# Seven block products in all four feed-forwards of a YOCO decoder step; state updates and gate sums at other places

## The chip, the cores and the metric

One core of a Trainium2 chip runs the whole program in one launch. The metric is the device time of one execution in microseconds (us), lower is better. Of each kernel there are several timed executions, and one profiled execution with a trace of every instruction on the five engines: PE (TensorE), DVE (VectorE), ACT (ScalarE), POOL (GpSimd), SP (SyncE, which here only issues DMAs).

## The reference

One inference step of a two-layer decoder, for 512 prompt tokens and 8 sequences of 4 new tokens. Layer 0 mixes by gated linear attention (GLA), layer 1 by forgetting attention (FoX) on keys and values that are projected once, after layer 0. Cut to what matters:

```python
D_MODEL, D_FF = 1024, 2816
def swiglu(u, w_up, w_down):
    a, b = jnp.split(u @ w_up, 2, axis=-1)
    return (jax.nn.silu(a) * b) @ w_down
for layer in range(2):
    mod = (silu(c) @ w_ada[layer] + b_ada[layer]).reshape(Bn, 3, 3, 1024)
    u = modulate(h, g[layer, 0], mod[:, 0, 0], mod[:, 0, 1])        # rmsnorm, scale, shift
    h = h + 0.5 * mod[:, 0, 2] * swiglu(u, w_ffn_up[layer, 0], w_ffn_down[layer, 0])
    u = modulate(h, g[layer, 1], mod[:, 1, 0], mod[:, 1, 1])
    h = h + mod[:, 1, 2] * (gla_mixer(u) if layer == 0 else fox_mixer(u, kv))
    u = modulate(h, g[layer, 2], mod[:, 2, 0], mod[:, 2, 1])
    h = h + 0.5 * mod[:, 2, 2] * swiglu(u, w_ffn_up[layer, 1], w_ffn_down[layer, 1])
    if layer == 0:
        kv = shared_kv(h, ...)              # K (normed), V and log forget values of all tokens
# GLA state of each sequence and head after its 4 tokens, 128 x 256:
#   S = exp(b_last) * S + k_decayed^T v
# FoX scores get cumulative sums of the log forget values
```

All is float32.

## The kernel before

The residual stream `h` stays in SBUF, features on partitions: `[128, 8, 544]`, 544 tokens = 512 + 32, worked on in two halves of 272. A float32 product is made of three matmuls on the high and low parts of both sides (`acc3`, L176 high x high, L177 low of the first x high, L178 high x low of the second); ACT makes the high parts by a cast (`halves`, L157), DVE the low parts by a subtraction (L158). So `u` lives as `uh` and `ul`, a weight as `hua` and `lua` and the like.

The program is one chain of stages. Times are from the trace, from the span's start: FFN "00" 31.4 to 475.8 us, GLA to 767, FFN "02" 768.2 to 1216.1, keys and values ("kv") 1217.9 to 1329.6, FFN "10" 1329.7 to 1733.3, FoX 1734.8 to 2036, FFN "12" 2037.4 to 2420.4, then the output.

An FFN has 22 pairs of 128 columns (`a` and `b` of SwiGLU). "00", "02" and "10" use `ffn`: for each pair and half, `pa` and `pb` (8 x 3 matmuls of 128x128 by 272 each), the gate, and the down products of groups of pairs (2, then 4 each), whose result `pd` is added into `h` with its gate (L393; the last 32 tokens by L396 and, on POOL, L398). "12" uses `ffn_seven`: the first 3 pairs as before, the other 19 by seven block products in place of eight. The operand of a pair is seen as a 2 x 2 block matrix (two halves of the features by two halves of the tokens) and the weights as 2 x 2 (features by `a` and `b`). Sums of blocks of `u` are made once, ahead of pair 3 (L534, L527; their high and low parts `th`, `tl`; the last of them is written over a quarter of `uh`, `ul` by `last_input`); sums of weights for each pair (`s`, L611, L612, L617, L618 on POOL); the seven products are combined on DVE and ACT (L643 to L680: `u`, `a`, `c`), and the gated result's low part `gl` is made on POOL (L649). Pairs go in rounds of 3, 3, 3, 3, 3, 3, 2, 2. While a round's products run, the down blocks of the round before are put between them (`between`); 16 blocks a round.

What else rides on the FFNs: "00" and "02" have the conditioning vectors (`ada_seq`, nine vectors each, matmuls `ada` in runs of 32 with their weight loads `adaw` of 512 KB on SP); "02" has also 16 `state_step`, which update the sample sequences' GLA states: two matmuls `pus` and two DVE updates `s` in each, with a masked key tile `km` (POOL) for every head, the state read by SP, and the result written by a DMA that POOL issues. "10" has four steps of gate work: logarithms of the forget gates (`gate_logs`, ACT), a transpose and running sum (`gate_turn`), sums at block borders (`gate_tiles`) and those of the cached pages (`gate_pages`). After the last block of a half, `after_half` makes the norm and the `u` of that half for the next stage (`nv`, `uh`, `ul`; L367, L386, L387).

In "kv", `proj_tokens` walks five chunks of columns by five token tiles (four of 128, one of the 32 samples), with the evacuation of a unit (norm of the keys, `hxk`, scaled on POOL, transposed on PE, split) one unit behind it.

The Tile framework's scheduler sets the order on each engine from the order of the code and of the dependences; tile pools with a count of buffers set how far ahead a load can run.

Of the kernel before, what the change touches and what calls it, by code (L numbers as in the profile page):

```python
# [99 lines left out]
def trunk_kernel(ctx: ExitStack, tc: tile.TileContext, a, out, dbg=None, stop=None):  # L100
# [19 lines left out]
    def raw_tile(name, dt=F32):  # L120
        return wp.tile([P, 1056], dt, tag="raw", name=name, bufs=4)

    def hi_tile(name, dt=F32R):
        return wp.tile([P, 1056], dt, tag="hi", name=name, bufs=6)

    def lo_tile(name, dt=F32R):
        return wp.tile([P, 1056], dt, tag="lo", name=name, bufs=6)
# [52 lines left out]
    def apply_u(ps, w, half, k0=0, k1=NB):  # L180
        t0, t1 = HALF[half]
        acc3(ps[:, 0:HA], [(w[0][:, k], w[1][:, k], uh[:, k, t0:t1], ul[:, k, t0:t1]) for k in range(k0, k1)], k0 == 0, k1 == NB)

# [147 lines left out]
    def spread(name, y, pieces):  # L331
        diag = tmp.tile([P, 3, P], F32, tag="diag", name=f"diag{name}", bufs=1)
# [175 lines left out]
    def ffn_seven(name, l, s, gate, after_half, steps=(), final=False, plain=3):  # L508
        wu = a["w_ffn_up"][l, s]
        wd = a["w_ffn_down"][l, s]  # L510
        steps = list(steps)
# [6 lines left out]
        with tc.tile_pool(name="ffn" + name, bufs=1) as fp:  # L518
            th, tl = ({i: fp.tile([P, H2, HA], F32R, name=f"t{x}{i}{name}") for i in (1, 2, 4)} for x in "hl")
            t3 = fp.tile([P, H2, HA], F32, name=f"t3{name}")  # L520
# [14 lines left out]

            def inputs():
                for k in range(H2):
                    x1, x2 = (tmp.tile([P, HA], F32, tag="nv", name=f"x{i}{name}_{k}", bufs=3)[:] for i in (1, 2))
                    x3 = t3[:, k]
# [6 lines left out]
                    minus(x3, x2, x3)  # L546
                    minus(x2, x2, x1)
                    halves(th[2][:, k], tl[2][:, k], x2)
                    x4 = tmp.tile([P, HA], F32, tag="nv", name=f"x4{name}_{k}", bufs=3)[:]
# [16 lines left out]
            def g_tiles(q):  # L566
                gt[q] = (fp.tile([P, T], F32R, tag="gh", name=f"gh{name}_{q}", bufs=6),
                         fp.tile([P, T], F32R, tag="gl", name=f"gl{name}_{q}", bufs=6))
# [8 lines left out]
            def plain_up(q, half):  # L577
                t0, t1 = HALF[half]
# [3 lines left out]
                apply_u(pb, wt[q][1], half)  # L582
                g = tmp.tile([P, HA], F32, tag="sq", name=f"g{name}_{q}_{half}", bufs=3)
                S.activation(g[:], pa[:, 0:HA], AF.Silu)
                V.tensor_tensor(out=g[:], in0=g[:], in1=pb[:, 0:HA], op=ALU.mult)
                halves(gt[q][0][:, t0:t1], gt[q][1][:, t0:t1], g[:])

# [63 lines left out]
            def seven(q, between):  # L651
# [32 lines left out]
                if steps:  # L684
                    steps.pop(0)()
# [34 lines left out]
            for q in range(2):  # L720
                plain_weights(q)
            plain_up(0, 0)
            plain_up(1, 0)
            plain_up(0, 1)
# [21 lines left out]
            for r in range(1, len(rounds)):  # L746
                todo = blocks(r - 1)
                n, done = 7 * len(rounds[r]), [0]

                def between():  # L750
                    done[0] += 1
                    while len_out[0] < 2 * NB * done[0] // n:
                        next(todo)
                        len_out[0] += 1
                len_out = [0]
# [4 lines left out]
            r = len(rounds) - 1  # L760
            for half in range(2):
                for m in range(NB):
                    down_block(r, m, half, True)
                    if half == 0 and m % 2 == 0:
                        down_weights(r, m // 2 + 1) if m < NB - 2 else None
                after_half(half)
# [92 lines left out]
    def proj_tokens(name, w2d, chunks, evac, evac_s, last=(0, 1, 4, 2, 3)):  # L859
# [28 lines left out]
        for ci, pieces in enumerate(chunks):  # L888
# [7 lines left out]
            for i, t in enumerate(order):  # L896
                if ci < len(chunks) - 1 and i == 3:
# [95 lines left out]
    def late_masks():  # L993
# [4 lines left out]
    ffn("00", 0, 0, mod(0, 0, 2), after("01", mod(0, 1, 0), mod(0, 1, 1)),  # L998
        seq0[:-2] + [late_consts, late_masks], first=(w00, feed), held=seq0[-2:])
# [5 lines left out]
    gsv = ExitStack()  # L1005
    gs_pool = gsv.enter_context(tc.tile_pool(name="gsv", bufs=1))
    vs = gs_pool.tile([P, 256], F32, name="vs")
    kts = gs_pool.tile([P, P], F32, name="kts")
    ebl = gs_pool.tile([P, 4, 12], F32, name="ebl")
# [315 lines left out]
    def state_stacks():  # L1325
# [13 lines left out]
    def state_step(hd, bh, pr):  # L1339
        if bh == 0 and pr == 0:  # L1340
            if hd == 0:
                state_stacks()
# [4 lines left out]
        if pr == 0:  # L1347
            t = gs_pool2.tile([P, 1024], F32, tag="s1", name=f"s1_{hd}_{bh}", bufs=1)
            stk["s"] = t[:].rearrange("p (b e) -> p b e", b=4)
            SP.dma_start(out=stk["s"], in_=a["state_gla"][0, 4 * bh:4 * bh + 4, hd].rearrange("b d e -> d b e"))  # L1350
        st = stk["s"]
# [6 lines left out]
        if pr:  # L1358
            G.dma_start(out=out[6][0, 4 * bh:4 * bh + 4, hd].rearrange("b d e -> d b e"), in_=st)

    with tc.tile_pool(name="gsv2", bufs=1) as gs_pool2:
        st_steps = [lambda hd=hd, bh=bh, pr=pr: state_step(hd, bh, pr) for hd in range(4) for bh in range(2) for pr in range(2)]
        seq = []
        seq1 = ada_seq(range(11, 20))
        for i, s in enumerate(seq1[:-2]):
            seq.append(s)
            if i >= 2 and st_steps:
                seq.append(st_steps.pop(0))
        ffn("02", 0, 1, mod(0, 2, 2), after("kv", 72, 80), seq + st_steps, held=seq1[-2:])
    gsv.close()  # L1370
# [43 lines left out]
    gates = ExitStack()  # L1414
    gt_pool = gates.enter_context(tc.tile_pool(name="gate", bufs=1))
    lf = gt_pool.tile([P, 5, 16], F32, name="lf")
    with tc.tile_pool(name="kvt", bufs=1) as kp:
# [39 lines left out]

        nv = {(hf, k): kp.tile([P, HA], F32, name=f"nv10_{hf}_{k}") for hf in range(1) for k in range(NB)}
        left = proj_tokens("kv", a["w_kvf"], [[(0, 512)], [(512, 512)], [(1024, 352)], [(1376, 352)], [(1728, 320), (2048, 16)]], evac_kv, evac_kvs, (4, 0, 1, 2, 3))
# [7 lines left out]
    le = gt_pool.tile([P, 5, 16], F32, name="le")  # L1467
    lt = gt_pool.tile([16, TP], F32, name="lt")
    rs = gt_pool.tile([16, TP], F32, name="rs")
    loc = gt_pool.tile([16, TP], F32, name="loc")  # L1470
    loc2 = gt_pool.tile([16, 2, TP], F32R, name="loc2")
    off = gt_pool.tile([16, 4, 4, 1], F32, name="off")
    off2 = gt_pool.tile([16, 2, 16], F32R, name="off2")
    gsm = gt_pool.tile([16, 16, P], F32, name="gsm")
    lp = gt_pool.tile([P, 2, 8, 16], F32, name="lp")
    lne = gt_pool.tile([32, 8, 16], F32, name="lne")

    def gate_logs():
        S.activation(le[:], lf[:], AF.Abs)
        S.activation(le[:], le[:], AF.Exp, scale=-1.0)  # L1480
        S.activation(le[:], le[:], AF.Ln, bias=1.0)
        V.tensor_scalar(out=lf[:], in0=lf[:], scalar1=0.0, scalar2=None, op0=ALU.min)
        V.tensor_tensor(out=lf[:], in0=lf[:], in1=le[:], op=ALU.subtract)
# [359 lines left out]
```

## Time and profile before

| | us |
|---|---|
| runs | 2422.88, 2429.81, 2434.22 (median 2429.81) |
| profiled execution | 2429.69, of it the span 2427.9; TensorE clock 0.989 of full |
| FFN "00", "02", "10" (plain) | 444.4, 447.9, 403.6 |
| FFN "12" (seven products) | 383.0 |
| GLA; FoX | 289; 301 |
| keys and values | 112 |

Rows in the profile read: line, engine, operation, tiles out<-in, shape, count | busy us, mean ns of one | idle time before them and what ended it. Rows of stretches give for each engine its busy us and instructions, the granted TensorE clock, the share of time in which the DMA engines were busy, and GB/s.

### The profile page before, as it was taken

The page shows a single profiled execution, that of the slowest core. Times are in us where ns is not written, and L with a number is a line of the kernel's source. Part 1 is how long each engine was busy: PE and PEld are TensorE (multiplying, and loading weights), DVE is VectorE, ACT ScalarE, POOL GpSimd, SP SyncE. Part 2 cuts the span into 40 slices and gives each one's busy share as a digit, 9 for nine tenths or more (in the row PEclk, how much of TensorE's full clock was granted, in tenths as well). Part 3 has the DMA queues.
Part 4 walks back from the last instruction along what each step waited for, and adds up shares of the span by engine and source line. Part 5 has one row for each costly group of instructions (what it writes and reads, how often), then busy time and mean ns, then how long its engine had stood idle before and what let it go on. Part 6 is the DMA issues. An engine that isn't in the chain of part 4 may idle for free.

```text
span 2427.9 us, 48518 instructions
## 1 busy us (share of the span) xinstructions
PE 2362.8 (97%) x19976; PEld 2215.4 (91%) x19976; DVE 1381.7 (57%) x3082; ACT 832.4 (34%) x1529; POOL 443.5 (18%) x574
## 2 busy tenths in 40 slices
PE   7999999998999999999999999999998899999999
PEld 6999999997979999999979999999896569999999
DVE  6343343548556453443585345344766666888887
ACT  3212222334534222221334323222435544444432
POOL 0000000206202010100120000000224212355442
PEclk8999999998999999999999999999999999999999
DMA  9636444322262645446337423222136751233322
GB/s 304 213 124 220 163 159 155 111 60 63 60 191 88 216 158 187 167 152 207 131 116 226 120 70 110 88 87 88 44 88 160 189 166 53 77 94 96 98 86 77
DMA packets 334131, 319.40 MB, mean 132 GB/s; under 512 B 24767, under 2 KB 287773, under 8 KB 333862
## 3 DMA queue, kind: packets, MB, share of 16 engines
q1 hardware_dynamic: 320134, 304.44, 39.5%
q0 software_dynamic: 13776, 11.87, 2.3%
q8 instruction: 157, 2.57, 0.4%
q14 instruction: 64, 0.52, 0.1%
HBM read 298.17 MB, written 18.38 MB: 130 GB/s over the span
## 4 chain that ended last, share of the span: by engine, by line
PE 82%; DVE 9%; DMA 4%; ACT 2%; POOL 2%; issue 1%; SPq 0%; ACTq 0%; DVEq 0%; POOLq 0%
PE pd L178 7%; PE pd L176 7%; PE pd L177 7%; PE pa L176 6%; PE pb L178 5%; PE pb L177 5%; PE pa L177 5%; PE pa L178 5%; PE pb L176 5%; PE p L177 3%; PE p L178 3%; PE p L176 3%; PE ada L231 3%; DMA kd<-khscr 2%; DVE nv L367 1%
## 5 line engine op out<-in xcount | busy, mean ns | idle before, releaser
L176 PE MATMUL pa<-uh,hua 128*128 128x272 f32 x1104 | 323.0, 293 | 1.8 <-ACT uh L386 1.7
L177 PE MATMUL pa<-ul,hua 128*128 128x272 f32 x1104 | 321.3, 291 | 0.4 <-DVE ul L387 0.2
L178 PE MATMUL pa<-uh,lua 128*128 128x272 f32 x1104 | 320.0, 290 | 0.0
L178 PE MATMUL pb<-uh,lub 128*128 128x272 f32 x1104 | 319.3, 289 | 0.0
L177 PE MATMUL pb<-ul,hub 128*128 128x272 f32 x1104 | 318.8, 289 | 0.0
L176 PE MATMUL pb<-uh,hub 128*128 128x272 f32 x1104 | 318.3, 288 | 0.0
L393 DVE SCALAR_TENSOR_TENSOR h<-pd,mods,h 128x272 f32<-128x272 f32 (+1 forms) x416 | 199.7, 481 | 194.8 <-PE pd L178 193.9
L178 PE MATMUL pd<-gh,lwd 128*128 128x272 f32 x1056 | 305.1, 289 | 0.0
L176 PE MATMUL pd<-gh,hwd 128*128 128x272 f32 x1056 | 305.0, 289 | 0.0
L177 PE MATMUL pd<-gl,hwd 128*128 128x272 f32 x1056 | 304.8, 289 | 0.0
L398 POOL TENSOR_TENSOR h<-h,gs 128x32 f32<-128x32 f32 x208 | 81.3, 391 | 941.4 <-DVE gs L396 936.0
L176 PEld LDWEIGHTS pa<-uh,hua 128*128 128x128 f32 x1104 | 208.9, 189 | 14.6 <-issue 6.0
L177 PEld LDWEIGHTS pa<-ul,hua 128*128 128x128 f32 x1104 | 209.3, 190 | 1.7 <-DVE ul L387 1.4
L178 PEld LDWEIGHTS pa<-uh,lua 128*128 128x128 f32 x1104 | 209.0, 189 | 0.0
L177 PEld LDWEIGHTS pb<-ul,hub 128*128 128x128 f32 x1104 | 209.0, 189 | 0.0
L176 PEld LDWEIGHTS pb<-uh,hub 128*128 128x128 f32 x1104 | 208.9, 189 | 0.0
L178 PEld LDWEIGHTS pb<-uh,lub 128*128 128x128 f32 x1104 | 208.7, 189 | 0.0
L446 DVE TENSOR_TENSOR g<-g,pb 128x272 f32<-128x272 f32 x132 | 57.7, 437 | 262.8 <-PE pb L178 261.4
L176 PEld LDWEIGHTS pd<-gh,hwd 128*128 128x128 f32 x1056 | 199.4, 189 | 1.7 <-issue 1.6
L177 PEld LDWEIGHTS pd<-gl,hwd 128*128 128x128 f32 x1056 | 199.3, 189 | 0.0
L178 PEld LDWEIGHTS pd<-gh,lwd 128*128 128x128 f32 x1056 | 199.1, 189 | 0.0
L157 ACT CAST hua<-rua 128x1024 fp32r<-128x1024 f32 x69 | 72.3, 1048 | 355.7 <-PE pd L177 264.2
(551 smaller groups left out, 5822.5 us busy)
## 6 DMA issues: line engine op xcount, KB each, us to landing
adaw<-in_w_ada_dram SPq DMA_DIRECT2D x128, 512.0 KB, 5.9
rua<-in_w_ffn_up_dram SPq DMA_DIRECT2D x88, 512.0 KB, 3.9
rub<-in_w_ffn_up_dram SPq DMA_DIRECT2D x88, 512.0 KB, 4.3
rwd<-in_w_ffn_down_dram SPq DMA_DIRECT2D x66, 512.0 KB, 5.0
rd<-in_w_ffn_down_dram SPq DMA_DIRECT2D x24, 384.0 KB, 3.3
adah<-in_w_ada_dram SPq DMA_DIRECT2D x16, 512.0 KB, 7.7
adaw<-in_w_ada_kv_dram SPq DMA_DIRECT2D x16, 512.0 KB, 6.4
s<-in_state_gla_dram SPq DMA_DIRECT2D x16, 512.0 KB, 4.4
```

Source lines behind the costliest of these rows:

```text
L157: S.copy(hi, src)
L176: PE.matmul(ps, lhsT=wh, rhs=xh, start=first and i == 0, stop=False)
L177: PE.matmul(ps, lhsT=wh, rhs=xl, start=False, stop=False)
L178: PE.matmul(ps, lhsT=wl, rhs=xh, start=False, stop=last and i == n - 1)
L231: PE.matmul(ps[32 * j:32 * j + 32, 0:256], lhsT=sc[:, k, :], rhs=t[:, j * 256:(j + 1) * 256], start=k == 0, stop=k == NB - 1)
L367: V.scalar_tensor_tensor(out=v[:, 0:p1 - t0], in0=h[:, k, t0:p1], scalar=mods[:, scale + k, 0:1], in1=rb[:, t0:p1], op0=ALU.mult, op1=ALU. ...
L393: V.scalar_tensor_tensor(out=h[:, m, t0:p1], in0=ps[:, 0:n], scalar=mods[:, gate + m, 0:1], in1=h[:, m, t0:p1], op0=ALU.mult, op1=ALU.add)
L398: G.tensor_tensor(out=h[:, m, TP:T], in0=h[:, m, TP:T], in1=st[:], op=ALU.add)
L446: V.tensor_tensor(out=g[:], in0=g[:], in1=pb[:, 0:HA], op=ALU.mult)
```

## The change

All four FFNs call `ffn_seven`. "00" and "02" call it with `slots=5` (tiles of gated results for five pairs, not six) and `late=True`: the fourth sum of blocks isn't kept from `inputs()` but made again in `last_input`, block by block. With `slots=5` the 16 down blocks of the last round are spread over the first 14 products of a round, so the first comes behind the first product, also in rounds with 21; with six, over all of a round's products. The conditioning steps are handed out by `tick()` after each product. The state updates go to "kv", one `state_step` a unit from the second on; the states are read through POOL's queue, two buffers ahead (`state_load`), the first two ahead of the stage. The gate work goes to FoX, to the units of its output gate. Smaller: raw, high and low weight tiles 1056 to 1040 wide, and the diagonal tile of `spread` shares a buffer.

Core of the diff:

```diff
-    def ffn_seven(name, l, s, gate, after_half, steps=(), final=False, plain=3):
+    def ffn_seven(name, l, s, gate, after_half, steps=(), final=False, first=None, held=(), slots=6, late=False):
...
+        total, ticks, n_ticks = len(steps), [0], 2 * plain + 7 * (NQ - plain)
+        def tick():
+            ticks[0] += 1
+            for _ in range(max(total * ticks[0] // n_ticks, min(total, ticks[0], 4)) - (total - len(steps))):
+                steps.pop(0)()
...
-            t3 = fp.tile([P, H2, HA], F32, name=f"t3{name}")
+            t3 = None if late else fp.tile([P, H2, HA], F32, name=f"t3{name}")
...
             def last_input():
-                S.copy(quarter(uh, 0, 1), t3[:])
-                minus(quarter(ul, 0, 1), t3[:], quarter(uh, 0, 1).bitcast(F32))
+                if not late:
+                    S.copy(quarter(uh, 0, 1), t3[:])
+                    minus(quarter(ul, 0, 1), t3[:], quarter(uh, 0, 1).bitcast(F32))
+                    return
+                for k in range(H2):
+                    x2, x3 = short(5, k), short(6, k)
+                    plus(x2, 1, 1, k)
+                    plus(x3, 0, 1, k)
+                    minus(x2, x2, x3)
+                    t0, t1 = HALF[1]
+                    halves(uh[:, k, t0:t1], ul[:, k, t0:t1], x2)
...
-                n, done = 7 * len(rounds[r]), [0]
+                n, done, gone = min(7 * len(rounds[r]), 7 * (slots - 3)), [0], [0]
...
-    def proj_tokens(name, w2d, chunks, evac, evac_s, last=(0, 1, 4, 2, 3)):
+    def proj_tokens(name, w2d, chunks, evac, evac_s, last=(0, 1, 4, 2, 3), extra=()):
...
             for i, t in enumerate(order):
+                if extra and ci + i:
+                    extra.pop(0)()
...
-    ffn("00", 0, 0, mod(0, 0, 2), after("01", mod(0, 1, 0), mod(0, 1, 1)),
-        seq0[:-2] + [late_consts, late_masks], first=(w00, feed), held=seq0[-2:])
+    ffn_seven("00", 0, 0, mod(0, 0, 2), after("01", mod(0, 1, 0), mod(0, 1, 1)),
+              seq0[:-2] + [late_consts, late_masks], first=(w00, feed), held=seq0[-2:], slots=5, late=True)
...
+    def state_load(gs_pool2, i):
+        if i < 8:
+            hd, bh = divmod(i, 2)
+            t = gs_pool2.tile([P, 1024], F32, tag="s1", name=f"s1_{hd}_{bh}", bufs=2)
+            stk["s", i] = t[:].rearrange("p (b e) -> p b e", b=4)
+            G.dma_start(out=stk["s", i], in_=a["state_gla"][0, 4 * bh:4 * bh + 4, hd].rearrange("b d e -> d b e"))
...
         if pr:
             G.dma_start(out=out[6][0, 4 * bh:4 * bh + 4, hd].rearrange("b d e -> d b e"), in_=st)
+            state_load(gs_pool2, 2 * hd + bh + 2)
...
-        ffn("02", 0, 1, mod(0, 2, 2), after("kv", 72, 80), seq + st_steps, held=seq1[-2:])
+    seq1 = ada_seq(range(11, 20))
+    ffn_seven("02", 0, 1, mod(0, 2, 2), after("kv", 72, 80), seq1[:-2], held=seq1[-2:], slots=5, late=True)
```

The rows of an engine's program in order, with the tile names' running numbers:

On DVE, the end of the head of a seven-product FFN, up to the first combination of products (`u_3`) and the first down result (`pd_0_0_0`). Before, in "12", with `t` the kept sum:

```order
L527 TENSOR_TENSOR t_23215<-x_3_23659,t_23215 128x272
L158 TENSOR_TENSOR lu_3_4_23682<-rua_3_23430,hu_3_4_23681 128x512
L527 TENSOR_TENSOR x_3_23659<-x_3_23659,x_3_23658 128x272
L158 TENSOR_TENSOR ld_0_0_23692<-rd_0_0_23689,hd_0_0_23691 128x768
L158 TENSOR_TENSOR tl_23213<-x_3_23659,th_23210 128x272
L585 TENSOR_TENSOR g_2_1_23643<-g_2_1_23643,pb_2_1_23618 128x272
L527 TENSOR_TENSOR x_3_23670<-x_3_23670,x_3_23659 128x272
L527 TENSOR_TENSOR ul<-t_23215,uh 128x4x272
L158 TENSOR_TENSOR gl_2_23429<-g_2_1_23643,gh_2_23428 128x272
L158 TENSOR_TENSOR tl_23214<-x_3_23670,th_23211 128x272
L158 TENSOR_TENSOR ld_0_1_23744<-rd_0_1_23741,hd_0_1_23743 128x768
L643 TENSOR_TENSOR u_3_23728<-p_3_23715,u_3_23700 128x272
```

The same place in the changed kernel, in "02" (L539 and L546 are the old L527 and L534):

```order
L546 TENSOR_TENSOR x_2_9926<-uh,ul 128x272
L546 TENSOR_TENSOR x_3_9932<-uh,ul 128x272
L539 TENSOR_TENSOR x_2_9925<-x_2_9925,x_2_9926 128x272
L612 TENSOR_TENSOR g_2_1_9880<-g_2_1_9880,pb_2_1_9855 128x272
L546 TENSOR_TENSOR x_3_9933<-uh,ul 128x272
L158 TENSOR_TENSOR ul<-x_2_9925,uh 128x272
L158 TENSOR_TENSOR gl_2_9641<-g_2_1_9880,gh_2_9640 128x272
L539 TENSOR_TENSOR x_3_9932<-x_3_9932,x_3_9933 128x272
L158 TENSOR_TENSOR ld_0_1_9991<-rd_0_1_9988,hd_0_1_9990 128x768
L158 TENSOR_TENSOR ul<-x_3_9932,uh 128x272
L398 SCALAR_TENSOR_TENSOR h<-pd_0_0_0_9977,mods,h 128x272
L671 TENSOR_TENSOR u_3_10007<-p_3_9994,u_3_9962 128x272
```

The one wide subtraction into `ul` has become four groups of two sums, a difference and a low part, and a down result now stands ahead of the first combination.

On POOL, the state updates before, inside "02": `km` the masked keys, the outputs, and the 32-token residual parts between them:

```order
L1344 TENSOR_TENSOR km_9176<-kstk,cst 96x1024
L1359 DMA out_dram<-s_0_0_9178 128x4x256
L398 TENSOR_TENSOR h<-h,gs_0_0_9679 128x32
L398 TENSOR_TENSOR h<-h,gs_0_1_9698 128x32
L398 TENSOR_TENSOR h<-h,gs_0_2_9717 128x32
L398 TENSOR_TENSOR h<-h,gs_0_3_9736 128x32
```

And in the changed kernel, at the start of "kv" (`hxk` is the keys' scaling, L1393 the load of a state, which waits for the output of the state two before it):

```order
L1450 TENSOR_TENSOR hxk_0_15184<-hxk_0_15184,gk 128x512
L1400 TENSOR_TENSOR km_15238<-kstk,cst 96x1024
L1411 DMA out_dram<-s_0_0_15121 128x4x256
L1400 TENSOR_TENSOR km_15499<-kstk,cst 96x1024
L1450 TENSOR_TENSOR hxk_1_15272<-hxk_1_15272,gk 128x512
L1393 DMA s_1_0_15298<-in_state_gla_dram 128x4x256
L1411 DMA out_dram<-s_0_1_15123 128x4x256
L1393 DMA s_1_1_15421<-in_state_gla_dram 128x4x256
L1450 TENSOR_TENSOR hxks_15335<-hxks_15335,gk 128x128
L1450 TENSOR_TENSOR hxk_2_15395<-hxk_2_15395,gk 128x512
L1411 DMA out_dram<-s_1_0_15298 128x4x256
L1450 TENSOR_TENSOR hxk_3_15458<-hxk_3_15458,gk 128x512
```

The state's outputs, loads and masked keys have moved from among the residual parts to among the key scalings, in the queue that issues both.

On ACT, the tail of "10" in the changed kernel, where the squares `sq` of the norm, the row sums' copy `rb` and the first `uh` of FoX stand:

```order
L351 ACTIVATE sq_4_21471<-h 128x272
L1528 ACTIVATE le<-lf 128x80
L1529 ACT_TABLE_LOAD
L1529 ACTIVATE le<-le 128x80
L351 ACTIVATE sq_5_21489<-h 128x272
L344 COPY rb<-rb_21389 128x272
L351 ACTIVATE sq_6_21507<-h 128x272
L351 ACTIVATE sq_7_21524<-h 128x272
L1530 ACT_TABLE_LOAD
L1530 ACTIVATE le<-le 128x80
L391 ACTIVATE uh<-nv_0_0_21438,mods 128x272
```

Before, the three `le` rows and their table loads stood in the first ten microseconds of "10"; now they stand here.

More of the change, by code (lines that the diff above doesn't have):

```diff
@@ L763, in ffn_seven @@
                     down_block(r, m, half, True)
-                    if half == 0 and m % 2 == 0:
-                        down_weights(r, m // 2 + 1) if m < NB - 2 else None
-                after_half(half)
+                    if half == 0 and m % 2 == 0 and m < NB - 2:
+                        down_weights(r, m // 2 + 1)
+                    if half and m >= 2 and us_:
+                        us_.pop(0)()
+                if held:
+                    held.pop(0)()
+                while us_:
+                    us_.pop(0)()
+                us_ = after_half(half) or []
             for s_ in steps:
@@ L1002, in trunk_kernel @@
         return
[L1005 to L1009, printed above, removed]
     def gla(after_half):
@@ L1412, in norm_heads @@
         return fin
[L1414 to L1417, printed above, removed]
+    lf = kvp.tile([P, 5, 16], F32, name="lf")
+    with ExitStack() as es:
+        kp = es.enter_context(tc.tile_pool(name="kvt", bufs=1))
         gk = kp.tile([P, 64], F32, name="gk")
```

213 lines of the change are left out of this document (118 added, 95 removed).

## Prediction

> **What bounds the kernel now.** I read the page first (engines, slices, chain), then windows per stage, then waits, then the groups of two stages. Durations are of the one profiled execution: 2429.69 us, a span of 2427.9 and 1.8 around it; the median of the runs is 2429.81, so sums need no shift.
>
> ```profile
> PE 2362.8 (97%) x19976; PEld 2215.4 (91%) x19976; DVE 1381.7 (57%) x3082; ACT 832.4 (34%) x1529; POOL 443.5 (18%) x574
> PE 82%; DVE 9%; DMA 4%; ACT 2%; POOL 2%; issue 1%; SPq 0%; ACTq 0%; DVEq 0%; POOLq 0%
> ```
>
> TensorE is busy 97% and is 82% of the chain that ends last: a matmul left out is time saved, unless another engine cannot follow. Whether one can is read by stage:
>
> ```profile
> 1329.66:1733.29 403.63, 403.45 (x3206) 402.63 (x3204) 182.61 (x348) 112.90 (x186) 25.26 (x57) 1.00 0.29 87
> 2037.41:2420.36 382.95, 378.39 (x2980) 376.67 (x2980) 323.13 (x594) 151.93 (x264) 167.97 (x176) 0.99 0.28 85
> 2090.00:2412.00 322.00, 320.82 (x2556) 320.60 (x2556) 268.33 (x468) 127.22 (x214) 154.96 (x160) 1.00 0.30 88
> 800.00:1196.00 396.00, 395.77 (x3353) 378.95 (x3352) 166.91 (x308) 93.07 (x151) 30.25 (x55) 1.00 0.52 177
> ```
>
> The columns are stretch, sum, PE, PEld, DVE, ACT, POOL, clock, DMA share, GB/s. The first row is FFN "10", plain; the second FFN "12", which has the seven-product form already, and so stands for what the other three become. Its steady part (third row) runs at 322.00/2556 = 126.0 ns per matmul, the plain one at 403.63/3206 = 125.9: same pace. But DVE rises from 45% to 83% and POOL from 6% to 48%. The fourth row is the body of "02": no TensorE loss either, with conditioning vectors and state updates inside; DMA is at 0.52.
>
> **The change part by part.** *Products.* Plain: 22 pairs x 2 matrices x 8 blocks x 3 passes x 2 halves = 2112 up, 1056 down: 3168. Seven products: 3 plain pairs (288), 19 x 7 x 4 blocks x 3 = 1596, 1056 down: 2940. So 228 fewer in each, 684 in three: 684 x 125.9 ns = **-86.1 us**, all on the bounding engine. What feeds the rest is not free: the heads, round borders and tails of "12" are slower than its pace.
>
> ```profile
> 2049.44:2062.00 12.56, 12.00 (x93) 11.45 (x92) 11.53 (x30) 6.90 (x17) 1.50 (x2) 1.00 0.01 3
> 2062.00:2090.00 28.00, 25.91 (x193) 25.48 (x192) 26.70 (x54) 12.23 (x27) 6.46 (x4) 0.94 0.16 48
> PE p L176 <- ACT th L157: 1.8, 1, 1.8
> L534 DVE TENSOR_TENSOR x<-uh,ul 128x272 f32<-128x272 f32 x12 | 6.7, 587 | 0.0
> L527 DVE TENSOR_TENSOR x<-x,x 128x272 f32<-128x272 f32 x8 | 3.5, 432 | 0.0
> L158 DVE TENSOR_TENSOR tl<-x,th 128x272 fp32r<-128x272 f32 x12 | 5.4, 459 | 0.7 <-ACT th L157 0.7
> L231 PE MATMUL ada<-adaw,sc 128*32 128x256 f32 x514 | 31.6, 382 | 0.0
> ```
>
> *Heads.* These 40.56 us of "12" hold 286 matmuls, worth 36.0: 4.6 lost, with DVE 94% busy making the four input sums, and a clock of 0.94 in the second stretch. In "00" and "02" the last input is made anew (8 sums at .587, 4 differences at .432, 4 low parts at .459 = 8.3 us) in place of four differences and one wide subtraction (3.0 us by width): about +5.2 us of DVE. Against it stand three runs of conditioning matmuls that the order puts into each head, 32 x 61 ns (31.6 us / 514, in "02") = 2 us a run, 5.9 us, in which TensorE doesn't need DVE. So +4 each (0 to 10). In "10" half 0's inputs were prepared in the stage before: +1 (0 to 4.6). Heads: **+9**.
>
> ```profile
> PE pd L177 <- POOL gl L649: 1.2, 1, 1.2
> POOL s L611 <- DMA rub<-in_w_ffn_up_dram: 29.2, 9, 4.3
> L649 POOL TENSOR_TENSOR gl<-c,gh 128x272 fp32r<-128x272 f32 x34 | 32.1, 950 | 11.7 <-ACT gh L648 11.7
> L611 POOL TENSOR_TENSOR s<-rua,rub 128x512 f32<-128x512 f32 x19 | 26.3, 1387 | 44.2 <-DMA rub<-in_w_ffn_up_dram 29.2 <-ACT c L679 3.9 <-PE p L178 3.7
> ```
>
> *Round borders.* The one steady wait of "12" is at 2334.9, in a round of two pairs: the first down block comes right after one product and waits for the low part, which on POOL stands behind the weight sum (and that for its weights). With five slots every round of "00" and "02" is fed in 14 products, so all seven borders are like that: 0 to 7 x 1.2 = 8.4 us each. I take two waits, 2.5, since the low part is only late where the weights are. "10" is "12" in form: 1.5. Borders: **+6.5**.
>
> *Tails.* After half 0's last block TensorE has half 1's to cover the norm: 4 pairs x 8 x 3 = 96 matmuls now, 12.1 us; then 2 pairs, 48, 6.0 us.
>
> ```profile
> 1717.89:1738.80 20.91, 19.30 (x144) 17.95 (x142) 17.05 (x50) 9.45 (x20) 7.92 (x16) 1.00 0.08 25
> L1480 ACT ACT_TABLE_LOAD x1 | 1.3, 1283 | 0.0
> L1481 ACT ACT_TABLE_LOAD x1 | 1.3, 1283 | 0.0
> L1479 ACT ACTIVATE le<-lf 128x80 f32<-128x80 f32 x1 | 0.3, 265 | 0.0
> L1506 DVE COPY gsm<-off 16x2048 f32<-16x2048 f32 x2 | 2.4, 1208 | 0.0
> ```
>
> The first row runs from half 0's last block to the end of its inputs: 1.6 us idle, DVE 82%. TensorE comes 6 us sooner to what needs them; the next projection can start on the first of eight, so I take 2.5 for "00" and 1.5 for "10" (each 0 to 6); the tail of "02" is priced below. The gate logarithms now stand among the squares and u of "10"'s tail on ACT, with two table loads: 2.6 + 3 x .27 = 3.4 us, ACT being 45% busy: +2 (0 to 3.4). The other gate work goes from one TensorE-bound stage to another (8 small matmuls); its row sums and 2.4 us of copies meet FoX: +1. Tails and gates: **+7**.
>
> *State updates.* Out of "02" go 32 matmuls; at the pace of 126 ns about **-4 us**. They go to the keys and values:
>
> ```profile
> 1217.00:1237.00 20.00, 19.39 (x160) 15.10 (x153) 15.95 (x56) 6.76 (x16) 2.56 (x5) 0.91 0.06 8
> 1237.00:1257.00 20.00, 20.00 (x92) 16.35 (x91) 19.96 (x78) 8.17 (x13) 5.84 (x4) 1.00 0.49 155
> 1257.00:1277.00 20.00, 20.00 (x155) 16.82 (x155) 17.84 (x68) 6.53 (x11) 5.00 (x5) 1.00 0.65 193
> 1277.00:1297.00 20.00, 18.67 (x170) 17.16 (x168) 10.85 (x32) 5.24 (x9) 3.13 (x3) 1.00 0.87 257
> 1297.00:1317.00 20.00, 19.47 (x242) 18.63 (x243) 7.81 (x18) 5.75 (x10) 1.11 (x3) 1.00 0.62 187
> 1317.00:1331.00 14.00, 14.00 (x95) 14.00 (x94) 9.60 (x24) 10.32 (x22) 1.71 (x3) 1.00 0.98 296
> L1357 DVE SCALAR_TENSOR_TENSOR s<-s,ebl,pus 128x256 f32<-128x256 f32 x32 | 15.2, 475 | 0.0
> L1335 DVE CAST kstk<-kts 32x128 fp32r<-32x128 f32 x12 | 4.2, 353 | 0.2
> L1344 POOL TENSOR_TENSOR km<-kstk,cst 96x1024 fp32r<-96x1024 f32 x4 | 8.7, 2168 | 72.8 <-PE pus L1356 64.2 <-issue 8.6
> L1359 POOL DMA_DIRECT2D out_dram<-s x8 | 6.2, 780 | 162.6 <-DVE s L1357 128.2 <-DMA rwd<-in_w_ffn_down_dram 34.4
> DMA to landing us min/median/max: 3.2/3.2/5.5
> L1405 POOL TENSOR_TENSOR hxk<-hxk,gk 128x512 f32<-128x512 f32 x8 | 12.5, 1562 | 31.8 <-DVE hxk L1404 9.4 <-DVE h8w L152 8.5 <-DVE h2y L153 5.1
> ```
>
> DVE gets 15.2 + 4.2 = 19.4 us more, and is full already in 1237-1277. POOL gets 8.7 of km and 16 issues at .78 = 12.5, to its 19.4; a load waits in its queue for the landing of an earlier output (3.2 to 5.5 us, six times), and behind it wait the key scalings, for which the transposes wait. DMA carries 8.4 MB more, 28 us at the 296 GB/s of the last row, whose stretch is full. So kv costs from 4 (only the matmuls) to 28 us (all of the DMA, or DVE and part of POOL's, in the open); TensorE is idle for only 2.5 of these 114 us. I take the middle, **+16**, with "02"'s shorter tail inside: the 40 us in which DVE is full speak for the upper end, the last 54, where it is 52% busy, for the lower.
>
> On moving loads to POOL's queue the Trainium skill ("SBUF — State Buffer", section "SBUF: two separate sides", the box on the trap that DVE blocks DMA) warns that descriptors of such transfers are written by GpSimd and starve while DVE holds the shared port, 3100 ns where 620 is usual. By that factor, an estimate from the page, 16 issues would grow from 12.5 to 62 us and fill half of kv. The trace agrees only so far as 752 to 803 ns at a DVE share of 42% shows no starving; none shows it at 90%.
>
> Sum: -86.1 + 9 + 6.5 + 7 - 4 + 16 = -51.6, from 2429.7: **2378 us**. A check by whole stages: "12" took 20.7 us less than "10", of which 12 has a slow start of its own of some 2; 3 x 22.7 = 68, less the 16 + 3 and what "00" and "02" have beyond "12" (2), plus 4: -51.
>
> **The rivals.**
> A, kv is set by POOL and DVE: loads that wait in POOL's queue hold up the key scalings, so the stage grows by 28 to 40 instead of 16. For it: the blocking order, DVE at 19.96 of 20. Against: the room on DVE in the last 54 us. Gives 2390 to 2402, **2395**.
> B, every border of "00" and "02" waits: conditioning loads of 512 KB stand ahead of weights on SP, DMA at 0.52 there against 0.30 in "12". 14 borders x 1.2 to 2.4 us = 17 to 34 instead of 5: 2390 to 2407, **2397**. Against: six of nine waits for weights in "12" cost TensorE nothing.
> C, kv hides all but its matmuls, and heads are covered by conditioning: -12 and -8: **2358**.
> D, slower than before: DVE becomes the bound of "00" and "02". It decides from where an FFN's DVE work passes its TensorE work: 323 us in "12", 328 with the remade input, against 2940 x .126 + 514 x .061 = 402 us. DVE's operations would have to take some 22% longer to bind at all, and some 30% longer (434 us, 32 more in each) to eat the rest of the gain and the 12 us beyond it: **2442**. For it: more DMA and more writers beside them than in "12". Against: in the 396 us row DMA is at 0.52 already, and low parts and updates there last what they last elsewhere (475 ns for 256 columns).
> E, the saving isn't there: a product needs TensorE's pace, and the pace of "12" shows it is.
>
> **How the numbers follow.** The forecast 2378 (its own range 2366 to 2390) 0.5; A 0.19; B 0.13; C 0.11; D 0.03; several of A and B together, some 2420, 0.04. Leaving out D, the pair, and half of what lies beyond C's centre gives 2356 to 2404. A measurement of this kernel tells about 0.5% (12 us) from no change: below 2417.7 is faster: 0.93; within 0.04; slower 0.03.
>
> **What would show it.** Right: the three FFNs each 18 to 26 us shorter than now (the one of "02" with 4 more), DVE about 80% there, still no TensorE waits over 3 us but at heads and borders; kv some 16 us longer, with DVE near full. A shows as idle TensorE in kv ahead of transposes and of state products, POOL's queue waiting on its DMA; B as waits of down blocks for POOL's low parts, once per round; C as kv within 5 us of its old length. I am wrong if heads cost over 10 us each (DVE with the remade input, at half clock), or if the tail into GLA or kv idles for more than the 6 us that its cover lost.

## The result: 1% faster, half of what was forecast

The changed kernel takes 2403.56 us (median of four runs, 2399.89 to 2407.67), the kernel before 2428.97 (2422.88 to 2434.22): a ratio of 0.9897, 95% interval 0.9868 to 0.9925. It is 25 us faster; 51.6 were forecast. The time lies at the slow end of the stated range, 2356 to 2404. The profiled execution took 2402.91 us, 2401.1 of it the span, at a mean clock of 0.980 (0.989 before). The first lines of its page:

```profile
PE 2298.5 (96%) x19292; PEld 2141.6 (89%) x19292; DVE 1828.6 (76%) x3881; ACT 982.0 (41%) x1831; POOL 923.0 (38%) x960
```

TensorE has 684 matmuls fewer and is busy 64 us less. The steady parts keep the pace, as these stretches of "00", "02" and "12" show (columns as in the prediction):

```profile
95.00:440.00 345.00, 343.56 (x2939) 328.93 (x2939) 262.88 (x464) 129.04 (x219) 163.98 (x158) 1.00 0.51 166
800.00:1150.00 350.00, 348.72 (x2960) 334.69 (x2959) 274.15 (x486) 133.60 (x229) 166.55 (x159) 1.00 0.49 161
2063.00:2385.00 322.00, 321.34 (x2556) 321.12 (x2555) 270.26 (x468) 127.44 (x214) 154.63 (x160) 1.00 0.30 88
```

So the missing time is between them. I cut both traces at the first matmuls of the same work (the sample blocks of GLA's values and of FoX's queries are marks that stand after a tail, so each FFN has its tail with it) and set the forecast's terms beside the difference, in us:

| stretch | before | after | measured | forecast |
|---|---|---|---|---|
| FFN 00, to the samples block of GLA's values | 483.1 | 470.6 | -12.5 | -19.7 |
| rest of GLA | 253.7 | 251.8 | -1.9 | 0 |
| FFN 02, to the first matmul of kv | 449.7 | 419.5 | -30.2 | -26.2 |
| keys and values | 111.8 | 140.2 | +28.4 | +16 |
| FFN 10, to the samples block of FoX's queries | 419.4 | 402.6 | -16.8 | -22.7 |
| FoX's projections, with the gates | 90.8 | 93.2 | +2.4 | +1 |
| FoX's attention | 143.6 | 147.6 | +4.0 | 0 |
| the rest, with FFN 12 | 440.8 | 440.6 | -0.2 | 0 |

Three places miss: kv by 12, FFN 00 by 7, FFN 10 by 6. The experiments below also give the spread: in kernels in which a stretch was not touched, FFN 00 took 469.2 to 472.3, FFN 10 398.6 to 402.7, kv 137.7 to 146.2, FoX's attention 143.6 to 150.2. The 4 us of the attention are inside this spread, and nothing is read into them.

Much of what is missing is the clock. The trace records which clock TensorE was granted, 1.00 or 0.50. It was half for 7.2 us of FFN 00 before and 16.4 after, for 0 and 3.4 of FFN 02, for 3.4 and 17.1 of the keys and values, for 0 and 17.1 of FFN 10. If half of such time is lost, an estimate that holds where TensorE is the bound, that is 4.6, 1.7, 6.8 and 8.5 us more than before: 21.6 us, where the profiled execution misses by 24.8 and the other differences nearly cancel. Less this estimate, FFN 00 takes 461 to 463 us in each of the seventeen kernels with seven products below, whatever their time was.

**The keys and values after.** Waits of TensorE, engine, line and what was waited for, us in total, times, longest:

```profile
PE pus L1408 <- DVE s L1409: 8.6, 7, 2.8
PE pus L1408 <- POOL km L1400: 3.2, 2, 2.6
PE kv_s L962 <- POOL us L383: 2.7, 1, 2.7
PE pus L1408 <- DVE hssk L1447: 2.0, 1, 2.0
```

and three stretches of it:

```profile
1212.00:1232.00 20.00, 16.79 (x108) 12.65 (x106) 19.06 (x73) 2.96 (x5) 8.76 (x9) 1.00 0.64 188
1232.00:1252.00 20.00, 17.48 (x110) 13.78 (x110) 19.99 (x66) 6.14 (x10) 8.73 (x8) 1.00 0.87 269
1272.00:1292.00 20.00, 17.07 (x143) 16.10 (x142) 6.24 (x14) 2.97 (x6) 2.05 (x3) 0.83 0.63 219
```

DVE is full (19.99 of 20), TensorE waits with state products in its queue, and in the last of these stretches neither is full: it waits, and its clock falls to 0.83. The longest wait, 2.8 us up to 1277.3, is a chain: POOL waited 4.3 us for an output to land before it issued a state's load (1269.8), DVE's update waited 1.5 us for that load, and the product for the update; the clock was half from 1276.3 to 1283.1.

**The tail of FFN 10 after.** Two stretches from half 0's last block on, and the waits:

```profile
1679.00:1699.00 20.00, 14.67 (x82) 13.94 (x81) 11.16 (x39) 9.90 (x20) 11.80 (x21) 0.76 0.13 30
1699.00:1719.00 20.00, 19.51 (x131) 15.72 (x132) 15.15 (x57) 7.67 (x19) 2.86 (x4) 0.82 0.09 20
```

```profile
PE st L364 <- POOL sq L355: 3.5, 2, 1.9
PE rb L342 <- DVE diag L341: 1.9, 1, 1.9
```

Before, the 20.91 us from the same point held 19.30 us of TensorE at full clock. Now 82 matmuls stand in 20 us, and the clock falls.

**The head of FFN 00 after**, waits and two stretches.

```profile
PE pd L178 <- DVE ld L158: 2.8, 1, 2.8
PE pd L176 <- ACT hd L157: 2.5, 1, 2.5
```

```profile
75.00:90.00 15.00, 10.20 (x80) 9.76 (x78) 14.86 (x28) 6.60 (x14) 6.07 (x3) 0.95 0.68 215
90.00:105.00 15.00, 14.57 (x99) 14.57 (x100) 10.66 (x20) 4.75 (x9) 3.84 (x4) 0.82 0.22 67
```

The first down block comes behind the first product and waits for its weights (`hd`, `ld`) with DVE full; then the clock is down for some microseconds. The whole head, before and after, with the same conditioning work in both:

```profile
31.40:105.00 73.60, 73.31 (x690) 68.23 (x690) 37.34 (x69) 29.34 (x53) 0.91 (x2) 0.97 0.72 236
31.20:105.00 73.80, 68.24 (x611) 61.39 (x612) 62.48 (x128) 31.02 (x64) 15.10 (x12) 0.91 0.68 225
```

79 wide matmuls of 126 ns fewer fit into the same time: some 10 us are lost here.

### The profile page after: what moved, and what is told of

Read it like the earlier page. It is cut to its first block, busy times and chain, and to the rows that moved or that the text cites. A ratio compares the mean times of both kernels' runs of the same rounds, so it can differ in the third digit from the quotient of the medians.

```text
span 2401.1 us, 49301 instructions
## 1 busy us (share of the span) xinstructions
PE 2298.5 (96%) x19292; PEld 2141.6 (89%) x19292; DVE 1828.6 (76%) x3881; ACT 982.0 (41%) x1831; POOL 923.0 (38%) x960
## 5 line engine op out<-in xcount | busy, mean ns | idle before, releaser
L178 PE MATMUL pd<-gh,ld 128*128 128x272 f32 x1408 | 408.6, 290 | 3.3 <-DVE ld L158 3.3
L176 PE MATMUL pd<-gh,hd 128*128 128x272 f32 x1408 | 409.2, 291 | 2.5 <-ACT hd L157 2.5
L177 PE MATMUL pd<-gl,hd 128*128 128x272 f32 x1408 | 409.3, 291 | 2.2 <-POOL gl L677 2.2
L176 PE MATMUL p<-uh,hu 128*128 128x272 f32 x1216 | 351.8, 289 | 0.0
L177 PE MATMUL p<-ul,hu 128*128 128x272 f32 x1216 | 350.9, 289 | 0.0
L178 PE MATMUL p<-uh,lu 128*128 128x272 f32 x1216 | 350.8, 288 | 0.0
L158 DVE TENSOR_TENSOR lu<-rua,hu 128x512 fp32r<-128x512 f32 (+1 forms) x228 | 272.2, 1194 | 45.9 <-ACT hu L157 37.7
L178 PEld LDWEIGHTS pd<-gh,ld 128*128 128x128 f32 x1408 | 268.3, 191 | 3.9 <-DVE ld L158 3.9
L176 PEld LDWEIGHTS pd<-gh,hd 128*128 128x128 f32 x1408 | 268.4, 191 | 3.5 <-ACT hd L157 2.7
L177 PEld LDWEIGHTS pd<-gl,hd 128*128 128x128 f32 x1408 | 268.5, 191 | 3.0 <-POOL gl L677 3.0
## 6 DMA issues: line engine op xcount, KB each, us to landing
kp<-in_cache_k_dram SPq DMA_DIRECT2D x16, 512.0 KB, 11.9
```

The lines of the kernel that those rows point to most:

```text
L158: V.tensor_tensor(out=lo, in0=src, in1=hi.bitcast(F32), op=ALU.subtract)
L176: PE.matmul(ps, lhsT=wh, rhs=xh, start=first and i == 0, stop=False)
L177: PE.matmul(ps, lhsT=wh, rhs=xl, start=False, stop=False)
L178: PE.matmul(ps, lhsT=wl, rhs=xh, start=False, stop=last and i == n - 1)
```

## Experiments

All start from the changed kernel. Where only one profiled execution was taken, I read the stretch that was touched, against the spread above; whole times are given beside it.

**1. No state work.** The sample states' loads, products, updates and outputs are left out.

```diff
-        for i in range(2):
-            state_load(gs_pool2, i)
-        st_steps = [lambda hd=hd, bh=bh, pr=pr: state_step(...) ...]
+        st_steps = []
```

> The changed kernel without the GLA state updates (loads, products, updates and outputs of the sample states left out). The keys and values take 140.2 us in the changed kernel (1173.1 to 1313.4) and 111.8 before. Theory 1, the state work is what lengthens this stage: it falls to 114 to 118 us, and the whole to about 2378. Theory 2, the shorter tail of FFN 02 with its idle and half-clock stretches is most of it: it stays at 125 us or more, the whole at 2388 or more.

kv: 119.0 us (140.2 in the changed kernel), the whole 2383.00. The stage before, in the changed kernel and without state work:

```profile
1217.89:1329.66 111.77, 109.30 (x881) 96.41 (x877) 79.78 (x265) 40.81 (x75) 19.21 (x21) 0.98 0.59 176
1173.12:1313.35 140.23, 121.08 (x912) 104.38 (x909) 104.08 (x323) 48.69 (x95) 37.75 (x42) 0.94 0.65 201
1175.59:1294.62 119.03, 110.05 (x880) 96.58 (x877) 85.86 (x281) 44.12 (x83) 19.45 (x23) 0.99 0.54 164
```

The state work costs 21 us; the four other kernels without it in this stage (7, 8, 9 and the first of 15) have 116.5 to 118.0, so that with the spread of the untouched stage it is 19 to 30. 7 of the 28 are something else. From half 0's last down block of FFN 02 to kv's samples block the changed kernel has 34.7 us in which 23.0 are matmuls at their usual pace, the kernel before 35.9 with 29.0: 4.8 us more are lost in this tail, 3.4 of them inside the stage. The tail had been counted into kv's 16.

**2. Loads by SP.**

```diff
-            G.dma_start(out=stk["s", i], in_=a["state_gla"]...)
+            SP.dma_start(out=stk["s", i], in_=a["state_gla"]...)
```

> The changed kernel with the eight state loads issued by SP in place of POOL. Theory 1, TensorE in the keys and values waits for DVE (the updates must empty the shared bank before the next state product), and POOL's queue isn't the limit: the stage stays within 3 us of 140. Theory 2, POOL's queue, which waits 16 us for outputs to land and 6 us on issuing loads, holds the key scalings up: 8 us or more shorter. Theory 3, SP waits in its own queue for the outputs and the weight loads behind come late: 5 us or more longer.

kv: 134.2 us, 2399.47 in all. Between the first two theories, and below the whole spread of the untouched stage: POOL's queue is some 6 of the 21 us, 3.4 of them less time at half clock by the estimate. A load's time to landing was steadier, from POOL first and then from SP:

```profile
DMA to landing us min/median/max: 4.3/5.5/6.9
```

```profile
DMA to landing us min/median/max: 4.0/4.0/4.0
```

**3. FFN 10's last round of four pairs.**

```diff
-        for n in (3, 3, 3, 3, 3, 3, 2, 2):
+        for n in sizes:     # "10": (3, 3, 3, 3, 2, 2, 2, 4)
```

> FFN 10 alone with rounds of 3, 3, 3, 3, 2, 2, 2, 4 pairs, so that half 1's last blocks are 96 matmuls as before the change, not 48. Theory 1, the tail of FFN 10 loses its 12 us because the last blocks come twice as fast as squares and residuals and leave TensorE idle and at half clock: from half 0's last block to the projection's first samples block the loss falls from 15 us to about 5, the whole by 7 to 10, less some 2 for more borders. Theory 2, it is the gate logarithms and their table loads on ACT ahead of u: the loss falls by 3 us at most.

FFN 10 with its tail: 393.4 us (402.6), the whole 2399.25; the untouched keys and values took 146.2 in this execution. From half 0's last block to the samples block it is 31.2 us with 3.6 lost, before the change 31.2 with 3.5, in the changed kernel 37.3 with 15.4; the body of the FFN is 2.7 us longer in loss. There is no time at half clock in this FFN (17.1 us in the changed kernel). The waits and one stretch of the tail in this kernel, at full clock again:

```profile
PE st L364 <- POOL sq L355: 1.5, 1, 1.5
PE rb L342 <- DVE diag L341: 0.5, 1, 0.5
```

```profile
1675.00:1695.00 20.00, 19.50 (x158) 19.28 (x157) 12.09 (x36) 7.52 (x15) 8.33 (x12) 1.00 0.00 1
```

**4. Later first down blocks in FFN 00 and 02.**

```diff
-                    while gone[0] < min(2 * NB * done[0] // n, 2 * NB):
+                    d0 = done[0] if r > 1 or slots > 5 else max(0, (done[0] - 3) * 14 // 11)
+                    while gone[0] < min(2 * NB * d0 // n, 2 * NB):
```

> FFN 00 and 02 with the down blocks of their first seven-product round beginning after the third or fourth product, not after the first. Theory 1, the head of FFN 00 stalls because its first down weights are asked for before they can be there (their tile comes free only with the head's last weight part): the two waits (5 us) and the half clock behind them go, FFN 00 is 5 to 8 us shorter. Theory 2, DVE is the bound of the head and the wait only moves to the next combination: 2 us or less.

FFN 00: 466.9 us (470.6), FFN 02 420.8 (419.5), the whole 2398.82. Both waits for down weights are gone, but shorter ones stand in their place, on the remade input's parts (the wait of `pa` was there already):

```profile
PE p L177 <- DVE ul L158: 2.1, 2, 1.1
PE pa L176 <- ACT uh L391: 1.6, 1, 1.6
PE p L176 <- ACT uh L157: 1.3, 2, 1.0
```

3.7 us, between the theories; the three kernels with later first blocks (this one and the two of 15) have 466.5 to 468.0, against 469.2 to 472.3. What went is time at half clock, 10.0 us in FFN 00 against 16.4. Most of the waiting has moved to other parts that DVE makes.

**5. Gate logarithms back in FFN 10.**

> The gate logarithms alone put back into FFN 10 as its one step, so that they and their two table loads leave the tail of FFN 10. If the 3.4 us of ACT stand on the way to the first u, the loss from half 0's last block to the first samples block of the projection falls from 15.4 us to 12 or 13. If u waits for DVE's norm chain there anyway, it falls by under 1 us.

The edit makes `gate_logs` the only step of FFN 10. The tail's loss falls from 15.4 to 13.5, near what was expected of ACT on the way to u. But from half 0's last block to the samples block it takes 35.4 us, and in the ten kernels with the changed kernel's FFN 10 it takes 34.1 to 37.3: the fall isn't shown to come from the logarithms. The FFN's body loses 3.6 more, the stretch is 404.2 us, the whole 2403.89. The 2 us that the forecast gave them stay open, and moving them back returns nothing.

**6. Last rounds of four pairs in 00 and 02 too** (3, 3, 3, 3, 3, 2, 1, 4 there).

> Last rounds of four pairs in FFN 00 and 02 (3, 3, 3, 3, 3, 2, 1, 4) and in 10 (3, 3, 3, 3, 2, 2, 2, 4). FFN 10 with its tail as in the run of it alone, 9 us shorter. If the same cause works in 00 and 02, their tail losses fall from 11.0 to about 7.5 and from 11.7 to about 7 us, against which the rounds of one and two pairs cost 2 to 3 each: 2391 in all. If the conditioning matmuls held back for these tails cover them already, 00 and 02 become longer by those 2 to 3 us and the whole stays at 2396 to 2399.

FFN 10: 391.7 us, as in 3. FFN 00: 473.5 (470.6), FFN 02: 422.8 (419.5). The whole 2396.89. In 00 and 02 it loses 3 each, 1 to 4 against the untouched kernels (469.2 to 472.3, 419.0 to 421.8): the second theory.

**7. State updates in FFN 10** (one buffer, loads by SP, five slots, the input remade).

```diff
+        ffn_seven("10", ..., st10, slots=5, late=True)    # st10: a load, two steps, a pause, eight times
```

> The state updates in FFN 10 in place of the keys and values, spread over its products, loads by SP into one buffer; FFN 10 with five slots and the last input made anew, to have the room. The keys and values fall by 21 us as in the run without state work, to 119. If a DVE that is some 90% busy still follows, FFN 10 grows by the 4 us of the matmuls and 1 to 3 of the remade input: 2387 to 2390. If DVE becomes the bound there, it grows by 10 to 20 and the whole stays at 2395 or more.

kv falls to 117.9 us, FFN 10 grows from 402.6 to 430.6; the whole 2408.73. The state work, with the remade input and the five slots that make room for it, cost 28 us there, more than in kv.

**8. All of 4, 6 and 7 together:**

> State updates in FFN 10, last rounds of four pairs in 00, 02 and 10, and the later first down blocks in 00 and 02, all together. If the three causes are separate, their gains add: 15 and 12 and 4 us from 2403, about 2372. If they work on the same stretch (DVE, above all in FFN 10), 2380 or more.

2417.70 us: FFN 10 434.7. The gains didn't add, and FFN 10 is longer than in 7. That the state updates and the smaller rounds meet on DVE would explain it; no run shows it.

**9. State updates beside FoX's output gate**, one after each half block.

> The state updates beside FoX's output-gate blocks, one after each half block, where DVE is about half busy; loads by SP, tiles taken from the weight tiles. FoX's projections (first samples block to first score) take 93 us in the changed kernel, the keys and values fall by 21 as without state work. If the price of the updates is set by the room on DVE, FoX's projections grow by 4 to 8 us: about 2389. If it is a price of TensorE waiting for its updates wherever they stand, they grow by 20 or more, as FFN 10 did (28): 2403 or more.

kv 117.6, FoX's projections 109.5 (93.2): +16, the whole 2401.50. Cheaper than anywhere else, dearer than the room on DVE promised: TensorE waits 7.2 us for the first update, and the last 33 us of the stretch run at 0.97 and 0.66 of the clock:

```profile
PE pus L1408 <- DVE s L1409: 7.2, 1, 7.2
```

```profile
1743.00:1763.00 20.00, 19.36 (x141) 19.11 (x142) 10.31 (x17) 5.05 (x12) 4.77 (x4) 0.90 0.60 173
1763.00:1783.00 20.00, 19.60 (x155) 19.21 (x154) 13.87 (x28) 6.96 (x15) 4.82 (x5) 1.00 0.78 223
1783.00:1803.00 20.00, 17.12 (x127) 16.13 (x126) 9.22 (x31) 10.49 (x21) 8.38 (x11) 0.97 1.07 253
1803.00:1816.00 13.00, 10.43 (x47) 7.35 (x47) 8.21 (x20) 5.80 (x16) 10.37 (x9) 0.66 0.60 187
```

**10. Only in kv's last 16 units** (`if extra and 5 * ci + i >= 9`).

> The state updates in the keys and values, but only in the last 16 units (the values), where DVE was half busy before the change and the key norms are done. If DVE's room sets the price, the stage falls from 140 to about 128 us, less what the transfers of 8.4 MB cost where the queues were 60 to 98% busy (to 134). If it is the DMA queues, no gain or a loss.

kv: 151.3 us, 11 longer than in the changed kernel, the whole 2410.76; 27 us of the stage were at half clock (17.1 there). DVE's room doesn't set the price alone. POOL waited for outputs to land before it could issue the next loads, and DVE for the loads:

```profile
  DMA out_dram<-s: 25.9, 6
...
  DMA s<-in_state_gla_dram: 5.0, 3
```

With two buffers, a state's load, four updates and output are a chain; squeezed into fewer units it comes nearer to the bound. That is argued from these waits; no run has a third buffer.

**11. A PSUM bank of their own for the state products.**

> The changed kernel with a PSUM bank of their own for the state products in the keys and values, not one shared with the transposes. If the loss is the hand-over of the shared bank, TensorE's waits there fall and the stage is 5 to 10 us shorter. If it is that DVE has more work than the stage has time for, the waits only change place: within 3 us of 140.

kv: 141.0 us, 2403.04: no change.

**12 to 14. What part of the state work costs.** In the order of the changed kernel the second product of each step waits for the first update. One run puts both products first:

```diff
         for i in range(2):
             ...
             PE.matmul(o, lhsT=stk["m"][:, b], rhs=stk["v"][:, hd], start=True, stop=True)
+        for i in range(2):
+            ...
             V.scalar_tensor_tensor(out=st[:, 2 * pr + i], ..., in1=o, ...)
```

> The changed kernel with both products of a state step ahead of both updates. In the order of the changed kernel the second product of each step waits for the first update, as both stand in one PSUM bank, and DVE's queue is long there. If this hand-over is the price of the updates in the keys and values, TensorE's 14 us of waits there fall below 6 and the stage (140.2 us) by 6 to 12. If the price is DVE's work, the waits go elsewhere: 3 us at most.

One leaves the products out (the updates add a fixed tile):

> The changed kernel without the 32 state products: the updates add a fixed tile in SBUF, so DVE has all its updates, POOL its masks and the queues their transfers, but TensorE never waits for them (the sample states are not the right ones). If the hand-over is the price, the stage falls to 120 to 124 us. If DVE's work is the price, it stays at 132 or more.

One leaves the updates out:

> The changed kernel without the 32 updates: products, masks, loads and outputs stay, 15 us of DVE go, and no product waits for an update (the sample states go out as they came in). Either theory brings the stage down to 120 to 126 us; if it stays at 130 or more, it is the transfers, or POOL's masks and queue.

kv: 136.4 us with both products first (whole: 2397.07), 140.4 without products (2406.08), 131.7 without updates (2387.56). Without any product TensorE cannot wait for an update, and the stage is as long as ever. The waits have moved to the next thing that DVE makes; first the waits of TensorE without products, then without updates:

```profile
PE kv L975 <- DVE lkv L158: 11.6, 5, 4.0
PE kv_s L962 <- POOL us L383: 3.8, 1, 3.8
```

```profile
PE pus L1408 <- POOL km L1400: 7.4, 2, 7.2
PE kv_s L962 <- POOL us L383: 3.4, 1, 3.4
```

So the hand-over isn't the price, though it is what the list of waits shows on top. The stage times can't simply be subtracted, since the clock differs. The stage without products, then without updates:

```profile
1174.50:1314.86 140.36, 119.40 (x880) 103.38 (x877) 107.18 (x327) 49.46 (x97) 39.37 (x42) 0.91 0.65 202
1168.56:1300.25 131.69, 119.27 (x912) 104.98 (x909) 92.67 (x292) 48.62 (x95) 38.52 (x42) 0.91 0.69 213
```

By the estimate 12 us were lost to half clock in each of these, 8.5 in the changed kernel and 1.7 without state work. Less that, the stage is 131.7 us in the changed kernel (127 to 135 in the kernels that leave it untouched), 128.4 without products, 119.7 without updates and 117.3 without state work. So DVE's updates are the largest part of the price, the half clock behind the waits is some 7 us of the 21, and what masks, copies, products and transfers add, single executions don't resolve. The 3.8 us of the pair's order lie hardly outside the stage's spread and aren't counted as shown.

**15. Two combinations.** State updates in FoX, with 3, and with 4 in FFN 00 alone:

> State updates in FoX's output-gate blocks, a last round of four pairs in FFN 10, and the later first down blocks in FFN 00 alone. If the three gains stand beside each other: 2403 less 14, 9 and 4, about 2376. If the updates cost in FoX what they cost in FFN 10, 2395 or more.

2390.08 us (2382.24 to 2390.32, five runs), 0.9818 of before (0.9800 to 0.9836), between the two expectations. And state updates kept in kv, loads by SP and both products first, with 3, and 4 in FFN 00:

> The changed kernel with both products of a state step ahead of its updates, state loads by SP, a last round of four pairs in FFN 10 and the later first down blocks in FFN 00. With the hand-over as the price: keys and values 12 to 15 us shorter, FFN 10 nine and 00 four: about 2377. With DVE's work as the price: keys and values 6 shorter, about 2384.

2380.07 us (2378.53 to 2383.25, five runs), 0.9781 of before (0.9766 to 0.9796): better than both kernels, and between the two theories. kv is 132.2 us, FFN 10 391.2, FFN 00 468.0.

## Why the prediction was wrong

- **Bound and products: right.** TensorE is the bound, its steady pace with seven products holds in "00" and "02" beside the conditioning, and the 684 matmuls are gone from its time. Rivals D and E are out.
- **The clock: a term put at nothing.** The sum prices each wait by its length. It named half clock as a sign of heads gone wrong, and saw 0.94 in the head of "12", but has no term for the time at half clock behind a wait. By the estimate above that is 21.6 of the missing 24.8 us, in the three places below above all.
- **Keys and values: the step that failed, by size.** "I take the middle, +16": it was 28.4, with FFN 02's tail at first inside the 16. State work is 21 us, some 7 of it half clock, and the tail 3.4; the rest is within the stage's spread. The measured 28.4 lies at the top of the range (4 to 28), and the row of full DVE was read rightly; the choice of the middle was not right. "The last 54, where it is 52% busy" were taken as room, but state work put there alone cost more (run 10). This is rival A by its size and its signs (POOL waited 16.3 us for outputs to land); of A's mechanism, POOL's queue, run 2 shows 6 of the 21 us. Rival C is out.
- **The tail of FFN 10: the second step that failed.** 1.5 and 2 us were forecast, 11.9 measured (8.7 to 11.9 over the ten kernels with this FFN). The cover was counted (48 matmuls for 96), the pace wasn't: with two pairs a block of half 0 comes every 0.75 us, and POOL takes 0.77 to add each block's square to the sum (L355, 768 ns), so the sums of the norm come late and TensorE waits for them, 3.5 us. The inverse root on DVE is read late, with weights' low parts of 1.2 us in between, 1.9 us more. The rest is mostly clock: it was half from 1682.5 to 1689.3 and from 1696.2 to 1706.4, by the estimate 8.5 of the 15.4 us lost. Four pairs take it all back (run 3); whether the logarithms on ACT had a part stays open (run 5).
- **The head of FFN 00: +4 forecast, some 10 measured** (79 wide matmuls fewer in the first 74 us). The forecast had DVE's remade input against conditioning runs, but not the order that puts a down block behind the first product, where its weights are late. Run 4 shows that part, 3.7 us; that the remainder is the remade input isn't shown. No run keeps the fourth sum in "00". "02" has the same order and stalls nowhere in its head.
- **Borders: +6.5 forecast, nearly nothing measured.** TensorE waited for low parts 0.5, 0.4 and 0.6 us in the steady parts of 00, 02 and 10; the 1.2 us of "12" aren't a price of each border. Rival B is out.
- **The Trainium skill's rule on POOL's queue.** The Trainium skill ("SBUF — State Buffer", section "SBUF: two separate sides") says that a transfer issued by GpSimd starves while DVE holds the shared port. Issuing took 748 to 811 ns for the loads and 757 to 800 for the outputs, with DVE at 19.99 of 20 us in part of the stage, against 752 to 803 in FFN 02: by issue times, no starving here. That SP's loads land in 4.0 us and POOL's in 5.5 goes in the rule's direction, by 1.5 us, not by a factor of five.

## What to carry to other kernels

A product that is saved on the bounding engine is paid for where stages meet: price the last blocks by the pace of the work that follows each (residual, square, sum), not by the time that they cover, and keep a long round for the end. Price a wait on the bounding engine with what comes behind it: in the changed kernel each stretch at half clock, up to the span's last 4 us, lasted 3.4, 6.8 or 10.2 us, so that a gap of 1.5 us cost more after it than in it. Work that was free beside an idle engine isn't free at 80 or 90% of it; before moving it, take its price from the stage's whole, by leaving it out, since the wait on top of the list (here the hand-over of products) can vanish without the stage getting shorter.

## What was not expected of the hardware

In the tail of FFN 10 TensorE had a gap of 1.5 us (1679.9 to 1681.4). From 1.1 us after it, its clock was half, for 6.8 us:

```profile
1679.90:1681.40 1.50, 0.00 (x0) 0.00 (x0) 0.21 (x2) 0.68 (x2) 1.42 (x3) 1.00 0.02 5
1681.40:1682.40 1.00, 0.99 (x8) 0.99 (x9) 0.00 (x0) 0.00 (x0) 0.16 (x1) 1.00 0.00 0
1682.50:1685.30 2.80, 2.80 (x17) 2.80 (x15) 0.47 (x1) 1.29 (x2) 0.00 (x0) 0.50 0.00 0
```

In the keys and values it fell 1.8 us into a gap:

```profile
1274.50:1276.30 1.80, 0.01 (x1) 0.00 (x0) 0.83 (x1) 1.13 (x2) 0.14 (x1) 1.00 1.04 376
1276.40:1277.30 0.90, 0.00 (x0) 0.00 (x0) 0.50 (x2) 0.00 (x0) 0.00 (x0) 0.50 1.17 411
```

The Trainium skill ("TensorE: Matmul & The Clock Gate", section "Part 1: The HAM clock gate (the "warmup" mystery)") gives about 3.4 us of idle time as the condition; in these two places 1.5 and 1.8 us were enough.
